# Attention in whole row groups instead of halves, in an encoder layer on one Trainium2 core

## The chip, the core and the metric

The kernel runs on one core of a Trainium2 chip. The core has a matrix engine (TensorE, PE in the profile; its weight loads are PEld), a vector engine (VectorE, DVE), a scalar engine (ScalarE, ACT), GpSimd (POOL) and a queue that issues DMA transfers (SyncE, SP). TensorE writes its results into PSUM, which has eight banks; VectorE and ScalarE read them from there, GpSimd works on SBUF. Each engine runs its own instructions in the order in which they were written, and waits at semaphores for the others. The metric is the device time of one execution in microseconds (us), the median of several runs.

## What is computed

One layer: RMS normalisation, a projection to queries, keys, values and a gate, neighbourhood attention on a grid of 32 rows by 64 columns, a SiLU gate, an output projection, the residual and a last normalisation. D_MODEL is 1024, SEQ 2048, with 16 heads of 64.

```python
h = rmsnorm(x, g)
q, k, v, gate = jnp.split(h @ w_in, 4, axis=-1)
# for each row r of the grid and each block of 16 columns: 8 rows x 32 columns of keys
s = jnp.einsum('bnqhd,bknjhd->bhnqkj', qr, kr) * scale
s = jnp.where(col_valid, s + bias, NEG_INF)
p = jax.nn.softmax(s, axis=-1)
o = jnp.einsum('bhnqkj,bknjhd->bnqhd', p, vr)
x = x + (o * jax.nn.silu(gate)) @ w_out
return rmsnorm(x, norm_f)
```

## The kernel before

**Stages.** The first half of the span is dense matrix products: values, and most of the projections in a seven-product scheme (`stage_one`, `stage_two`). Then comes attention, with the remaining dense matmuls fed in between its steps: first those of the projections (`projections`, lines 368 to 372, tiles `pp`), then those of the output projection (`outputs`, lines 1259 to 1263, tiles `po`). What is left of the output projection runs alone at the end. Dense products are made of three matmuls each, with operands split into a high and a low part.

**Attention's units.** Two heads are a pair p, eight pairs in all. The grid's rows are cut into four row groups T of eight rows; each sees the key rows `KEY_ROWS[T]`: 11, 15, 15 and 12 rows. The order is all pairs with T = 0, then for each pair T = 1 and T = 2, then all pairs with T = 3: 32 steps (p, T), called cycles below. Columns are cut into four groups C of 16 queries' columns with 24 or 40 key columns, the outer ones 24. A *half* is two column groups (0 and 1, or 2 and 3), so there are 64 halves, numbered i; N is 64.

**Steps of a half.** `scores(i)` makes 12 matmuls: two column groups, two heads, three products. Each head of a column group has a bank `s`. VectorE adds the table `EM` (bias and mask) and finds the largest value (line 1004, the masked sum), and ScalarE takes exponentials and their sums (line 1007). `normalise(i)` takes reciprocals on VectorE (line 1013) and scales on GpSimd (line 1015). `turns(i)` transposes the probabilities in 22 transposes of 64 x 64 results (line 1034) into two banks `ph` for each column group; ScalarE and VectorE copy these to SBUF tiles `pta` (lines 1037, 1038). `values(i)` makes 14 products, which the trace shows as 28 records (line 1052), into one bank `o` for each cycle. Behind a cycle's last half VectorE multiplies by the gate (line 1068) and the result is stored.

**The order around it.** The order is written out by hand. Step i of the loop at the end issues loads (`begin`), feeds dense matmuls in portions (`feed`, with `amount[i]` as the number of matmuls), and then one run without dense matmuls in it: `turns(i - 2)`, `scores(i)`, `values(i - 2)`, with `normalise(i - 1)` ahead of them. Later work (evacuations, stores, loads) stands in a list with a due time, counted in dense matmuls, and is issued when `due` passes it. A bank is handed out again when its readers are done, so a matmul that starts a new bank can wait for the copy of an older one.

**Tables.** `bias` (line 964) makes six tables `EM` for a pair on GpSimd, from two tiles `E` of bias rows (`load_e`, pool `ep`) and the mask. For T = 0 they change in each cycle, for T = 1 and 2 in every second one; for T = 3 they are loaded ready-made (`load_last`).

Of the kernel before, what the change touches and what calls it, by code (L numbers as in the profile page):

```python
# [69 lines left out]
def build(ctx, tc, x, xr, xt, wg, rpb, last, w_out, n0, nf, masks, out):  # L70
# [19 lines left out]
    qp = pool("qp", 4)  # L90
# [12 lines left out]
    pa = pool("pa", 2)  # L103
    mp = pool("mp", 6)
    ep = pool("ep", 4)
# [441 lines left out]

    X2 = {}
# [4 lines left out]
    def stage_one():  # L553
        us = [("k", j) for j in range(4)] + [(k, j) for j in range(4) for k in "qg"]
        X1 = {f: [(xs([128, 512], F32R, "h"), xs([128, 512], F32R, "l")) for _ in range(4)]
              for f in ("B12", "B11", "B21", "B22")}
        spot = mkp([128, 3, 512], F32, "spot")
        land = {f: [p([128, n], F32, "land")[:, :512] for _ in range(4)]
                for f, p, n in (("x12", kp, 960), ("x22", qp, 512), ("x11", vh, 512))}
        land["x21"] = [spot[:, k] for k in range(3)] + [lp([128, 512], F32, "land")]  # L560
        slots = [(mp, 512)] * 6 + [(ep, 512)] * 2 + [(sp, 512)] * 2 + [(pa, 768)] * 2 + [(vh, 512)] * 4
        slots += [(qp, 512)] * 4 + [(kp, 960)] * 4
# [4 lines left out]
        def split(f, t, k, scale=None):  # L567
            if f == "T1":
                X1.setdefault(f, []).append((xs([128, 512], F32R, "h"), xs([128, 512], F32R, "l")))
            elif f[0] == "T":  # L570
                X1.setdefault(f, []).append(tuple(p([128, n], F32R, "t")[:, :512] for p, n in (slots.pop(0), slots.pop(0))))
            split_to(*X1[f][k], t, scale and gain(scale, k))
# [191 lines left out]
    def stage_two():  # L764
        x12, x11, x21 = L2["x12"], L2["x11"], L2["x21"]
        x22 = [qp([128, 512], F32, "land") for _ in range(4)]
        for k in range(4):
            load_x(2, "x22", k, x22[k])
        slots = {"T2": [(mp, 512)] * 4 + [(kp, 960)] * 4,
                 "T3": [(sp, 512)] * 2 + [(pa, 768)] * 2 + [(qp, 512)] * 3 + [(lp, 512)],  # L770
                 "T4": [(vh, 512)] * 4 + [(mp, 512)] * 2 + [(ep, 512)] * 2}
# [65 lines left out]
        def form(f, x, *ks):  # L837
            def g():
                for k in ks:
                    h, l = (p([128, n], F32R, "t")[:, :512] for p, n in slots[f][2 * k:2 * k + 2])  # L840
# [126 lines left out]
    def load_last(p):  # L967
        if p % 2:
            ts = [mp([128, 512], F32, "em") for _ in range(6)]
        else:  # L970
            m = mkp([128, 3, 512], F32, "em")
            ts = [ep([128, 512], F32, "em") for _ in range(4)] + [m[:, 0], m[:, 1]]
# [11 lines left out]
    def scores(i):  # L984
# [14 lines left out]
        for C, pst in got:  # L999
            n = (r1 - r0) * width(C)  # L1000
            ST[i, C] = st = tiny.tile([128, 6], F32, name="st")
            X[i, C] = [xp([128, 512], F32, f"x{s}")[:, :n] for s in range(2)]
            for s in range(2):
                nc.vector.tensor_tensor_reduce(X[i, C][s], pst[s], EM[p, ROW_TYPE[T], COL_TYPE[C], s], -1.0, 1e38,  # L1004
                                               OP.add, OP.min, st[:, s:s + 1])
            for s in range(2):
                nc.scalar.activation(X[i, C][s], X[i, C][s], AF.Exp, bias=st[:, s:s + 1], scale=-1.0,  # L1007
                                     accum_out=st[:, 2 + s:3 + s])

    def normalise(i):  # L1010
        for C in pairs[i][2]:
            st = ST.pop((i, C))
            nc.vector.reciprocal(st[:, 4:6], st[:, 2:4])  # L1013
# [267 lines left out]
    first = 8  # L1281
# [141 lines left out]
```

## Time and profile before

| | |
|---|---|
| median of 3 runs | 1081.04 us (1079.96 to 1081.69) |
| the profiled execution | 1081.33 us, of which the span of its instructions is 1079.5 us |
| granted TensorE clock of that execution | 0.998 |
| dense stages, 0 to 535 us | TensorE busy 532.67 us |
| T = 0, 535 to 642 us | TensorE busy 105.83 us, GpSimd 64.36 us |
| T = 1 and 2, 642 to 870 us | TensorE busy 228.00 us, VectorE 159.78 us, ScalarE 147.44 us, GpSimd 114.88 us |
| T = 3, 870 to 1022 us | TensorE busy 151.69 us, VectorE 100.65 us |
| rest, 1022 to 1079.5 us | TensorE busy 49.80 us |

The span is divided by stages here, from a view that gives each engine's busy time in a stretch. Matmuls are pipelined and their ends are modelled: a record of a 512-column matmul is 0.39 us long while the next one starts 0.23 us after it, so start times say more than lengths. In a timeline several like records that follow each other are one row, with the start of the first and the end of the last.

### The profile page before, as it was taken

The page shows a single profiled execution, that of the slowest core. Times are in us where ns is not written, and L with a number is a line of the kernel's source. Part 1 is how long each engine was busy: PE and PEld are TensorE (multiplying, and loading weights), DVE is VectorE, ACT ScalarE, POOL GpSimd, SP SyncE. Part 2 cuts the span into 40 slices and gives each one's busy share as a digit, 9 for nine tenths or more (in the row PEclk, how much of TensorE's full clock was granted, in tenths as well). Part 3 has the DMA queues.
Part 4 walks back from the last instruction along what each step waited for, and adds up shares of the span by engine and source line. Part 5 has one row for each costly group of instructions (what it writes and reads, how often), then busy time and mean ns, then how long its engine had stood idle before and what let it go on. Part 6 is the DMA issues. An engine that isn't in the chain of part 4 may idle for free.

```text
span 1079.5 us, 21403 instructions
## 1 busy us (share of the span) xinstructions
PE 1068.0 (99%) x7621; PEld 872.9 (81%) x7621; DVE 721.4 (67%) x1695; ACT 520.1 (48%) x1245; POOL 278.4 (26%) x393
## 2 busy tenths in 40 slices
PE   9999999999999999999999999999999999999997
PEld 6888888887888888888878888888888888888885
DVE  5376888768897635566665667656777777676554
ACT  7545344333334334332366656665677655555321
POOL 0000222312321000000166665455445522222100
PEclk9999999999999999999999999999999999999999
DMA  8633555344545333424888777886888798876442
GB/s 304 223 98 101 191 203 183 126 133 138 175 132 150 109 88 102 162 96 143 275 254 274 216 241 232 256 253 193 259 291 261 211 284 276 257 240 203 133 147 78
DMA packets 129042, 207.59 MB, mean 192 GB/s; under 512 B 11752, under 2 KB 55272, under 8 KB 128936
## 3 DMA queue, kind: packets, MB, share of 16 engines
q1 hardware_dynamic: 128792, 205.97, 61.4%
q8 instruction: 60, 0.98, 0.4%
q14 instruction: 46, 0.38, 0.1%
q10 hardware_dynamic: 144, 0.26, 0.1%
HBM read 147.47 MB, written 58.72 MB: 191 GB/s over the span
## 4 chain that ended last, share of the span: by engine, by line
PE 95%; DVE 3%; ACT 1%; issue 1%; POOL 0%; DVEq 0%; POOLq 0%; ACTq 0%
PE pp L424 29%; PE pv L545 16%; PE o L1052 8%; PE s L997 8%; PE po L1263 6%; PE po L1259 6%; PE po L1261 5%; PE ph L1034 4%; PE pp L372 4%; PE pp L368 4%; PE pp L370 4%; DVE f L407 1%; PE zp L1278 1%; ACT x L1007 0%; DVE raw L413 0%
## 5 line engine op out<-in xcount | busy, mean ns | idle before, releaser
L1015 POOL TENSOR_SCALAR x<-x,st 128x360 f32<-128x360 f32 (+5 forms) x256 | 142.3, 575 | 270.2 <-DVE st L1013 225.0
L424 PE MATMUL pp<-h,f 128*128 128x512 f32 x576 | 186.3, 389 | 0.0
L1007 ACT ACTIVATE x<-x,st 128x360 f32<-128x360 f32 (+5 forms) x256 | 151.8, 594 | 50.3 <-DVE st L1004 50.1
L424 PE MATMUL pp<-t,f 128*128 128x512 f32 x648 | 156.0, 389 | 0.3 <-DVE u L437 0.2
L424 PEld LDWEIGHTS pp<-t,f 128*128 128x128 f32 x648 | 121.5, 188 | 26.3 <-DVE u L437 1.2
L444 POOL TENSOR_TENSOR tmp<-tmp,rb 128x512 f32<-128x512 f32 x36 | 58.5, 1626 | 271.8 <-DVE tmp L442 223.6
L1004 DVE CUSTOM_DVE_ANT_0 x<-s,em 128x360 f32<-128x360 f32 (+5 forms) x256 | 124.0, 540 | 3.9 <-PE s L997 2.6
L964 POOL TENSOR_TENSOR em<-e,mk 128x264 f32<-128x264 f32 (+3 forms) x94 | 77.1, 853 | 191.6 <-DVE u L437 189.8
L424 PEld LDWEIGHTS pp<-h,f 128*128 128x128 f32 x576 | 108.1, 188 | 22.3
L424 PE MATMUL pp<-l,f 128*128 128x512 f32 x288 | 112.0, 389 | 0.0
L1038 DVE COPY pta<-ph 120x384 f32<-120x384 f32 (+5 forms) x128 | 63.2, 517 | 66.6 <-PE ph L1034 66.2
L1037 ACT ACTIVATE pta<-ph 120x384 f32<-120x384 f32 (+5 forms) x128 | 52.1, 459 | 102.4 <-PE ph L1034 102.4
L1263 PE MATMUL po<-wol,gh 128*128 128x512 f32 x252 | 100.1, 397 | 0.0
L1259 PE MATMUL po<-woh,gh 128*128 128x512 f32 x252 | 99.4, 394 | 0.0
L1261 PE MATMUL po<-woh,gl 128*128 128x512 f32 x252 | 98.8, 392 | 0.0
L1052 PEld LDWEIGHTS o<-pta,vt 120*64 120x64 f32 (+2 forms) x1792 | 83.5, 137 | 18.5 <-issue 13.9
L1052 PE MATMUL o<-pta,vt 120*64 120x128 f32 (+5 forms) x1792 | 92.3, 254 | 0.3 <-ACT pta L1037 0.3
L545 PE MATMUL pv<-wh,h 128*128 128x512 f32 x256 | 88.2, 390 | 0.0
L545 PE MATMUL pv<-wh,l 128*128 128x512 f32 x256 | 87.9, 389 | 0.0
L545 PE MATMUL pv<-wl,h 128*128 128x512 f32 x256 | 87.9, 389 | 0.0
L997 PE MATMUL s<-kt,qh 64*128 64x480 f32 (+5 forms) x512 | 85.9, 377 | 1.2 <-DVE st L1004 1.0
L407 DVE TENSOR_TENSOR f<-raw,f 128x512 fp32r<-128x512 f32 x90 | 69.7, 775 | 22.4 <-ACT f L406 22.4
(147 smaller groups left out, 1874.4 us busy)
## 6 DMA issues: line engine op xcount, KB each, us to landing
raw<-in_wg_dram SPq DMA_DIRECT2D x126, 256.0 KB, 4.6
row<-in_xr_dram SPq DMA_DIRECT2D x32, 256.0 KB, 4.8
vd<-v SPq DMA_DIRECT2D x32, 256.0 KB, 2.9
k_hi<-hi SPq DMA_DIRECT2D x32, 256.0 KB, 3.0
k_lo<-lo SPq DMA_DIRECT2D x32, 256.0 KB, 3.1
sgd<-sg SPq DMA_DIRECT2D x32, 256.0 KB, 2.8
qr<-qd SPq DMA_DIRECT2D x32, 256.0 KB, 5.9
sgt<-sgd SPq DMA_DIRECT2D x32, 256.0 KB, 7.0
```

The costliest lines, as they stand in the source:

```text
L407: nc.vector.tensor_tensor(t[:, 1], src, t[:, 0].bitcast(F32), OP.subtract)
L424: nc.tensor.matmul(B[n, P], t[:, int(m == 2), c], x[k][int(m == 1)], start=P in (1, 6, 5) and k == 0 and m == 0, stop=k == 3 and m == 2, s ...
L545: nc.tensor.matmul(ps[t], a[:, o], b, start=k == 0 and m == 0, stop=k == NK - 1 and m == 2)
L964: (nc.gpsimd if attending[0] or not s else nc.vector).tensor_tensor(sh(t), E[p, s][:, u0 + 4:u1 + 4, v0 + 8:v1 + 8].rearrange("p u (s v) - ...
L997: nc.tensor.matmul(pst[s], qq[a, qs], kk[a, :r1 - r0, c0:c1].rearrange("p r (s c) -> p s r c", c=8), start=(m == 0), stop=(m == 2))
L1004: nc.vector.tensor_tensor_reduce(X[i, C][s], pst[s], EM[p, ROW_TYPE[T], COL_TYPE[C], s], -1.0, 1e38, OP.add, OP.min, st[:, s:s + 1])
L1007: nc.scalar.activation(X[i, C][s], X[i, C][s], AF.Exp, bias=st[:, s:s + 1], scale=-1.0, accum_out=st[:, 2 + s:3 + s])
L1015: nc.gpsimd.tensor_scalar(X[i, C][s], X[i, C][s], st[:, 4 + s:5 + s], 0.5, op0=OP.mult, op1=OP.mult)
L1052: nc.tensor.matmul(o[s * 64:s * 64 + 64, C * 128 + q0:C * 128 + q0 + nq], vt[:k, strip, s * 64:s * 64 + 64], t[:k, at:at + nq], start=firs ...
L1259: nc.tensor.matmul(p, gh, woh[q, j], start=(i == 0), stop=False)
L1261: nc.tensor.matmul(p, gl, woh[q, j], start=False, stop=False)
L1263: nc.tensor.matmul(p, gh, wol[q, j], start=False, stop=(i == NK - 1))
```

## The change

`turns`, `scores` and `values` of a whole cycle now stand in one run, and the loop goes over cycles m instead of halves i. Its run is: the transposes of both halves of cycle m - 1 (44), the scores of both halves of cycle m (24 matmuls), the values of both halves of cycle m - 1. The portion of dense matmuls between two runs is 28 for the first 25 steps and some 53 for the others, in place of 14 and 23 between two halves.

- The turned probabilities of a cycle lie in one tile `pta` of 3072 columns (`pt`, one buffer, in place of `pa` with two of 768). They come out of six banks: for each half two of 512 columns, one for each 64 queries, and two of 384 that both halves share. Each bank is copied whole, three by ScalarE and three by VectorE, so 96 copies by each in place of 128.
- `normalise` of a cycle's first half stands within `scores` of its second, between the masked sums of its two column groups; `normalise` of the second half stands 45% into the next portion of dense matmuls. Each takes one reciprocal for four sums in place of two.
- The table sums on GpSimd (`tables`) stand behind that normalising, 65% into the portion, in place of at its start. The pool of bias rows has two buffers in place of four, and the rows for the next tables are asked for behind the values of a run.
- Loads of keys, queries, values and gates have other places in the portion. `qp` has two buffers in place of four, and the first two stages use other tiles as landing places and operands (`xp`, the sixths of `pt`, `qp`).
- `run_roots` runs in each cycle.

```diff
     raw = pool("raw", 6)
     kp = pool("kp", 4)
-    qp = pool("qp", 4)
+    qp = pool("qp", 2)
     vp = pool("vp", 2)
     vhalf = []
...
     sp = pool("sp", 2)
     xp = pool("xp", 8)
     mkp = pool("mkp", 1)
-    pa = pool("pa", 2)
+    pt = pool("pt", 1)
     mp = pool("mp", 6)
-    ep = pool("ep", 4)
+    ep = pool("ep", 2)
+
+    def sixths():
+        t = pt([128, 3072], F32R, "sixths")
+        return [t[:, i * 512:i * 512 + 512] for i in range(6)]
+
...
               for f in ("B12", "B11", "B21", "B22")}
         spot = mkp([128, 3, 512], F32, "spot")
         land = {f: [p([128, n], F32, "land")[:, :512] for _ in range(4)]
-                for f, p, n in (("x12", kp, 960), ("x22", qp, 512), ("x11", vh, 512))}
+                for f, p, n in (("x12", kp, 960), ("x22", xp, 512), ("x11", vh, 512))}
+        sixth = sixths()
         land["x21"] = [spot[:, k] for k in range(3)] + [lp([128, 512], F32, "land")]
-        slots = [(mp, 512)] * 6 + [(ep, 512)] * 2 + [(sp, 512)] * 2 + [(pa, 768)] * 2 + [(vh, 512)] * 4
-        slots += [(qp, 512)] * 4 + [(kp, 960)] * 4
+        slots = [(mp, 512)] * 6 + [(qp, 512)] * 2 + [(sp, 512)] * 2 + sixth[:2] + [(vh, 512)] * 4
+        slots += sixth[2:] + [(kp, 960)] * 4
 
...
-    def scores(i):
+    def scores(i, between=None):
         p, T, cs = pairs[i]
         kh, kl = KT[p, T]
         qh, ql = QT[p, T]
@@ -996,72 +1007,109 @@
                     a = slice(s * 64, s * 64 + 64)
                     nc.tensor.matmul(pst[s], qq[a, qs], kk[a, :r1 - r0, c0:c1].rearrange("p r (s c) -> p s r c", c=8), start=(m == 0), stop=(m == 2))
             got.append((C, pst))
-        for C, pst in got:
+        ST[i] = st = tiny.tile([128, 12], F32, name="st")
+        for j, (C, pst) in enumerate(got):
             n = (r1 - r0) * width(C)
-            ST[i, C] = st = tiny.tile([128, 6], F32, name="st")
             X[i, C] = [xp([128, 512], F32, f"x{s}")[:, :n] for s in range(2)]
             for s in range(2):
+                o = 2 * j + s
                 nc.vector.tensor_tensor_reduce(X[i, C][s], pst[s], EM[p, ROW_TYPE[T], COL_TYPE[C], s], -1.0, 1e38,
-                                               OP.add, OP.min, st[:, s:s + 1])
+                                               OP.add, OP.min, st[:, o:o + 1])
+            if between and j == 0:
+                between()
             for s in range(2):
-                nc.scalar.activation(X[i, C][s], X[i, C][s], AF.Exp, bias=st[:, s:s + 1], scale=-1.0,
-                                     accum_out=st[:, 2 + s:3 + s])
+                o = 2 * j + s
+                nc.scalar.activation(X[i, C][s], X[i, C][s], AF.Exp, bias=st[:, o:o + 1], scale=-1.0,
+                                     accum_out=st[:, 4 + o:5 + o])
 
     def normalise(i):
-        for C in pairs[i][2]:
-            st = ST.pop((i, C))
-            nc.vector.reciprocal(st[:, 4:6], st[:, 2:4])
+        st = ST.pop(i)
+        nc.vector.reciprocal(st[:, 8:12], st[:, 4:8])
+        for j, C in enumerate(pairs[i][2]):
             for s in range(2):
-                nc.gpsimd.tensor_scalar(X[i, C][s], X[i, C][s], st[:, 4 + s:5 + s], 0.5, op0=OP.mult, op1=OP.mult)
+                o = 8 + 2 * j + s
+                nc.gpsimd.tensor_scalar(X[i, C][s], X[i, C][s], st[:, o:o + 1], 0.5, op0=OP.mult, op1=OP.mult)
 
     def split(C):
         return [b for b in strips(C) if b[3] == 128], [b for b in strips(C) if b[3] == 64]
 
-    def turns(i):
-        p, T, cs = pairs[i]
-        k = 8 * (KEY_ROWS[T][1] - KEY_ROWS[T][0])
-        for C in cs:
+
+
+    def places(m):
+        p, T = order[m]
+        put, at = {}, [1024, 1024]
+        for C in range(4):
             full, part = split(C)
-            halves_ = [full + [b for b in part if b[2] == 64 * h] for h in range(2)]
-            t = PT[i, C] = pa([128, 768], F32, "pta")
-            slots = t.rearrange("p (n h q) -> p h n q", h=2, q=64)
-            ph = [bank(384, f"ph{h}") for h in range(2)]
-            for j in range(3):
+            for b, blk in enumerate(full):
                 for s in range(2):
                     for h in range(2):
-                        if j < len(halves_[h]):
-                            o, at, q = j * 128 + s * 64, halves_[h][j][1] * k, slice(64 * h, 64 * h + 64)
-                            nc.tensor.transpose(ph[h][:k, o:o + 64], X[i, C][s][q, at:at + k], ident[q, q])
+                        put[C, blk[0], s, h] = C * 256 + b * 128 + s * 64
+            for blk in part:
+                for s in range(2):
+                    h = blk[2] // 64
+                    put[C, blk[0], s, h] = at[h]
+                    at[h] += 64
+        return put
+
+    def turns(m):
+        p, T = order[m]
+        k = 8 * (KEY_ROWS[T][1] - KEY_ROWS[T][0])
+        put = places(m)
+        PT[m] = t = pt([128, 3072], F32, "pta").rearrange("p (h c) -> p h c", h=2)
+        banks_ = {}
+
+        def copy(b):
+            w = (512, 512, 384)[b]
             for h in range(2):
-                n = len(halves_[h])
-                put = (lambda o, i_: nc.scalar.activation(o, i_, AF.Copy)) if h else nc.vector.tensor_copy
-                put(slots[:k, h, :2 * n], ph[h][:k, :128 * n].rearrange("p (n q) -> p n q", q=64))
+                (nc.vector.tensor_copy if h else lambda o, i_: nc.scalar.activation(o, i_, AF.Copy))(
+                    t[:k, h, b * 512:b * 512 + w], banks_[b, h][:k, :w])
+
+        for b in range(2):
+            for h in range(2):
+                banks_[b, h] = bank(512, f"ph{h}")
+            if b == 0:
+                banks_[2, 0], banks_[2, 1] = bank(384, "ph0"), bank(384, "ph1")
+            lists = [[], []]
+            for C in (2 * b, 2 * b + 1):
+                full, part = split(C)
+                for blks in (full, part):
+                    for blk in blks:
+                        for s in range(2):
+                            for h in range(2):
+                                if (C, blk[0], s, h) in put:
+                                    lists[h].append((put[C, blk[0], s, h], C, s, blk[1] * k))
+            for h in range(2):
+                lists[h].sort()
+            for n in range(max(len(l) for l in lists)):
+                for h in range(2):
+                    if n < len(lists[h]):
+                        o, C, s, at = lists[h][n]
+                        q = slice(64 * h, 64 * h + 64)
+                        nc.tensor.transpose(banks_[o // 512, h][:k, o % 512:o % 512 + 64], X[2 * m + b, C][s][q, at:at + k], ident[q, q])
+                if n == 7:
+                    copy(b)
+        copy(2)
 
     def values(i):
         p, T, cs = pairs[i]
         k = 8 * (KEY_ROWS[T][1] - KEY_ROWS[T][0])
+        put = places(i // 2)
         if cs[0] == 0:
             O[p, T] = bank(512, "o")
         o = O[p, T]
         vt = VT[p, T]
+        t = PT[i // 2]
         for C in cs:
             X.pop((i, C))
-
-        def product(C, s, blk, t, at, first, last):
-            strip, _, q0, nq = blk
-            nc.tensor.matmul(o[s * 64:s * 64 + 64, C * 128 + q0:C * 128 + q0 + nq],
-                             vt[:k, strip, s * 64:s * 64 + 64], t[:k, at:at + nq],
-                             start=first, stop=last, skip_group_check=True)
-
-        for C in cs:
             full, part = split(C)
-            for b, blk in enumerate(full):
+            for b, (strip, _, q0, nq) in enumerate(full + part):
                 for s in range(2):
-                    product(C, s, blk, PT[i, C], b * 256 + s * 128, b == 0, False)
-            for h, blk in enumerate(part):
-                for s in range(2):
-                    product(C, s, blk, PT[i, C], 512 + s * 128 + blk[2], False, h == len(part) - 1)
-            del PT[i, C]
+                    h = slice(q0 // 64, (q0 + nq) // 64)
+                    at = put[C, strip, s, h.start]
+                    to = o[s * 64:s * 64 + 64, C * 128 + q0:C * 128 + q0 + nq]
+                    nc.tensor.matmul(to.rearrange("d (h q) -> d h q", q=64) if nq > 64 else to,
+                                     vt[:k, strip, s * 64:s * 64 + 64], t[:k, h, at:at + 64] if nq > 64 else t[:k, h.start, at:at + 64],
+                                     start=b == 0, stop=b == len(full + part) - 1, skip_group_check=True)
...
-    early = 96 * (12 - len(units_two)) + 192
-    first = 8
-    kept = 60
-    amount = [(early - kept - 3 * first) / 48] * 48 + [(384 + kept - 30) / 18] * 18
-    calm_debt = amount[0] / 2
-    for i in range(3):
-        amount[i] += first
+    cycles = len(order)
+    dense, end_of_it = 28.0, 24
+    amount = [dense] * 25
+    first = 16
+    amount[0] -= first / 2
+    amount[1] += first
+    calm_debt = dense / 4
+    amount += [(96 * (12 - len(units_two)) + 546 - sum(amount) - first - end_of_it) / (cycles - 25)] * (cycles - 25) + [end_of_it]
     fill = projections()
     outs = outputs()
...
-    def begin(i):
+    def next_sums(m):
+        return next((n for n in range(m + 1, cycles) if order[n][1] < 2), None)
+
+    def begin(m):
         all_loads()
-        m = i // 2
         quiet[0] = True
-        if i % 2 == 0 and i < N:
-            p, T = order[m]
-            load_v(p, T)
-            ty = ROW_TYPE[T]
+        if m >= 1:
+            later_loads([lambda: load_sg(*order[m - 1])], 1, 0)
+        if m < cycles:
+            later_loads([lambda: load_v(*order[m])], 4, 0)
+        if m + 1 < cycles:
+            nx = order[m + 1]
+            if nx[1] == 3:
+                later_loads(load_last(nx[0]), 12, 1.5)
+            later_loads(load_k(*nx), 14 if nx[1] < 3 else 22, 5)
+        if m == 0:
+            bias(0, 0, 2)
+            later_loads(load_e(order[1][0]), 5, 3)
+
+    def middle(m):
+        if 1 <= m < cycles:
+            split_q(*order[m])
+        if m + 1 < cycles:
+            later_loads([load_q(*order[m + 1])], 1, 0)
+
+    def tables(m):
+        p, T = order[m]
+        ty = ROW_TYPE[T]
+        if (p, ty, 0, 0) not in EM:
             for cty in range(3):
-                if (p, ty, cty, 0) not in EM:
-                    bias(p, ty, cty)
-                    quiet[0] = i == 0
-            if m + 1 < len(order):
-                nx = order[m + 1]
-                kh, kl = load_k(*nx)
-                if nx[1] == 3:
-                    later_loads(load_last(nx[0]), 1, 1.5)
-                elif nx[0] != p:
-                    later_loads(load_e(nx[0]), 5, 3)
-                later_loads([kh, kl], 9, 4)
-        if i % 2 == 0 and 2 <= i <= N:
-            p, T = order[m - 1]
-            later_loads([lambda: load_sg(p, T)], 15, 0)
-
-    def middle(i):
-        m = i // 2
-        if i % 2 and m + 1 < len(order):
-            split_q(*order[m + 1])
-        if i == 0 or i % 2 and m + 2 < len(order):
-            later_loads([load_q(*order[m + (2 if i else 1)])], 1, 0)
+                bias(p, ty, cty)
+            quiet[0] = False
 
     stage_one()
     stage_two()
     attending[0] = True
-    for i in range(N + 2):
-        a = amount[i]
-        begin(i)
-        feed(a * 0.25)
-        if quiet[0]:
-            run_roots()
+    for m in range(cycles + 1):
+        a = amount[m]
+        begin(m)
+        feed(a * 0.15)
+        run_roots()
+        feed(a * 0.15)
+        middle(m)
+        feed(a * 0.15)
+        if m:
+            normalise(2 * m - 1)
         feed(a * 0.2)
-        middle(i)
-        feed(a * 0.55, 8)
-        if 0 < i <= N:
-            normalise(i - 1)
-        if i > 1:
-            turns(i - 2)
-        if i == N + 1:
+        if m < cycles:
+            tables(m)
+        feed(a * 0.35, 8)
+        if m:
+            turns(m - 1)
+        if m == cycles:
             all_loads()
             feed(6)
-        if i < N:
-            scores(i)
-        if i > 1:
-            values(i - 2)
+        else:
+            scores(2 * m)
+            if m == 0:
+                feed(first, 8)
+            scores(2 * m + 1, lambda: normalise(2 * m))
+        if m:
+            values(2 * m - 2)
+            values(2 * m - 1)
+        n = next_sums(m)
+        if 0 < m and n and order[m][1] < 2:
+            for f in load_e(order[n][0]):
+                f()
```

18 lines of the change are left out of this document (11 added, 7 removed).

## The prediction

> **What bounds the kernel now.** I read the page's busy times first, then its clock row and its chain of waits.
>
> ```profile
> span 1079.5 us, 21403 instructions
> PE 1068.0 (99%) x7621; PEld 872.9 (81%) x7621; DVE 721.4 (67%) x1695; ACT 520.1 (48%) x1245; POOL 278.4 (26%) x393
> PEclk9999999999999999999999999999999999999999
> PE 95%; DVE 3%; ACT 1%; issue 1%; POOL 0%; DVEq 0%; POOLq 0%; ACTq 0%
> ```
>
> TensorE is busy throughout, at full clock, and is 95% of the chain that ended last. So the time is the length of TensorE's own stream. The change neither adds nor removes a matmul, so its worth lies in how that stream is cut up. I therefore read the timeline of TensorE around one attention run of the middle stage (T = 1, 2); columns are start, length, engine, line, tiles, count.
>
> ```profile
> 747.64 0.39 PE L370 MATMUL pp<-l,w 128*128 128x512 f32 x1
> 747.87 0.39 PE L372 MATMUL pp<-h,w 128*128 128x512 f32 x1
> 748.19 0.80 PE L1034 MATMUL ph<-ident,x 64*120 64x64 f32 x20
> 748.91 0.74 PE L997 MATMUL s<-kt,qh 64*128 64x480 f32 x3
> 750.00 0.45 PE L997 MATMUL s<-kt,ql 64*128 64x360 f32 x2
> 750.38 1.44 PE L1052 MATMUL o<-pta,vt 120*64 120x128 f32 x28
> 751.43 0.39 PE L1052 MATMUL o<-pta,vt 120*64 120x128 f32 x5
> 751.75 0.50 PE L368 MATMUL pp<-h,w 128*128 128x512 f32 x1
> 752.09 0.40 PE L370 MATMUL pp<-l,w 128*128 128x512 f32 x1
> L1052 PE MATMUL o<-pta,vt 120*64 120x64 f32 x384 | 21.9, 221 | 0.0
> ```
>
> Dense matmuls follow each other every 0.23. The run takes 752.09 - 747.87 - 2 x 0.23 = 3.76 us beyond the dense stream. No engine wait stands in these rows, yet there are seams:
> - Entering: a dense matmul would have started at 748.10; the first transpose starts at 748.19: 0.09.
> - Leaving: the last five records of the values start at 751.43 and end at 751.82. A last one of 0.22 starts at 751.60, some 0.04 after the one before it. The first dense matmul starts 0.15 after it, and the second one 0.34 later instead of 0.23: 0.11 + 0.11 = 0.22.
> - Scores to values: the second score starts at 748.91 and the eleventh at 750.00, so 0.121 each; eleven would end at 750.24, and the values start 0.14 after that. The neighbouring run has the narrow column group first:
>
> ```profile
> 741.93 0.60 PE L997 MATMUL s<-kt,qh 64*128 64x360 f32 x3
> 742.91 0.56 PE L997 MATMUL s<-kt,ql 64*128 64x480 f32 x2
> 743.40 1.44 PE L1052 MATMUL o<-pta,vt 120*64 120x128 f32 x28
> ```
>
> There it is 0.109 each, and 743.40 - 741.93 - 11 x 0.109 = 0.27. A mean step overstates the seam where the wide group is last and understates it where it is first; their mean, 0.20, is what I use. From transposes to scores I see no seam.
>
> **The change, part by part.** *One run for two halves.* Before, 62 runs hold transposes, scores and values; in the changed program's order 31 runs hold 44, 24 and 28 products (56 records) with the same matmuls around them, and the dense total is the same. Each of the 31 saves one set of seams. Middle stage: 0.09 + 0.20 + 0.22 = 0.51. The first and last stage, one run each:
>
> ```profile
> 616.66 0.50 PE L997 MATMUL s<-kt,qh 64*128 64x264 f32 x3
> 617.40 0.42 PE L997 MATMUL s<-kt,ql 64*128 64x352 f32 x2
> 617.76 1.44 PE L1052 MATMUL o<-pta,vt 88*64 88x128 f32 x28
> 897.66 0.63 PE L997 MATMUL s<-kt,qh 64*128 64x384 f32 x3
> 898.55 0.39 PE L997 MATMUL s<-kt,ql 64*128 64x288 f32 x2
> 898.88 1.44 PE L1052 MATMUL o<-pta,vt 96*64 96x128 f32 x28
> ```
>
> T = 0, narrow first: 0.082 each, seam 0.20, less the 0.07 that the middle stage shows for this order: 0.13, in all 0.44. T = 3, wide first: 0.099 each, seam 0.13, plus 0.07: 0.20, in all 0.51. The first step among the transposes may be longer than the others too, by 0 to 0.05. I take 0.55, 0.47 and 0.54. With 16, 7 and 8 runs of scores: 8.8 + 3.3 + 4.3 = 16.4 us. Bounds: with the scores' seam at its smaller reading of 0.13 and no more, 13.5; with 0.27 and the long first step, 20. The last transposes and values, merged too, give 0.5.
>
> *Six banks and three wide copies on each engine, new waits.* All eight banks come around within a run: six turned banks, eight of scores and one of values, beside the dense one under way. In the new order each bank of scores after the first waits for a copy out of a turned bank, in turn ScalarE and VectorE. The last waits for the first masked sum on VectorE, and the values wait for the second. The copies of before:
>
> ```profile
> L1037 ACT ACTIVATE pta<-ph x128: 370/487/497, 549.5 to 1019.8; 120x384 f32<-120x384 f32 x48, 88x384 f32<-88x384 f32 x24, 96x384 f32<-96x384 f32 x24, 120x256 f32<-120x256 f32 x16
> L1038 DVE COPY pta<-ph x128: 400/547/558, 550.4 to 1019.9; 120x384 f32<-120x384 f32 x48, 88x384 f32<-88x384 f32 x24, 96x384 f32<-96x384 f32 x24, 120x256 f32<-120x256 f32 x16
> 748.79 1.02 DVE L1038 COPY pta<-ph 120x384 f32<-120x384 f32 x2 [1.47 <-PE ph L1034]
> 748.88 0.77 ACT L1037 ACTIVATE pta<-ph 120x384 f32<-120x384 f32 x2 [2.42 <-PE ph L1034]
> 750.04 0.66 DVE L1004 CUSTOM_DVE_ANT_0 x<-s,em 128x480 f32<-128x480 f32 x1 [0.23 <-PE s L997]
> 751.20 0.53 DVE L1004 CUSTOM_DVE_ANT_0 x<-s,em 128x360 f32<-128x360 f32 x1
> 751.65 0.53 DVE L1004 CUSTOM_DVE_ANT_0 x<-s,em 128x360 f32<-128x360 f32 x1
> ```
>
> 256 to 384 columns costs 0.117 on ScalarE and 0.147 on VectorE; a 512-wide copy is then 0.60 and 0.69 (estimates), each next one starting 0.08 earlier. 22 transposes take 748.91 - 748.19 = 0.72, a pair about 0.06. Before, twelve transposes are issued within 0.33 of the first, and copies start 0.27 (VectorE) and 0.36 (ScalarE) behind that. Now sixteen take 0.45. Times from the first transpose, T = 1, 2: ScalarE copies 0.81-1.41, 1.50-2.10, 2.02-2.50; VectorE 0.72-1.41, 1.41-2.10, 2.02-2.57; masked sums from 2.5 every 0.45 or 0.58. Transposes end at 1.43. First scores (360) 1.43-2.0: their second head needs 1.41, no wait. Second group needs ScalarE's second copy at 2.10, plus hand-over: wait 0.1. Third needs 2.50, has time until 2.75. Fourth, at 3.4, needs the first masked sum at 3.1. Values, at 4.0, need 3.5. So 0.1 per run. With T = 0 and 3 the first scores end 0.1 to 0.15 sooner against the same copies: 0.25. New waits: 16 x 0.1 + 15 x 0.25 = 5.4 us. Bounds: none, and 0.5 in each run, 15.5.
>
> [...]
>
> *Normalising and table sums moved.* The second half of a cycle is now normalised 12.6 dense matmuls (2.9 us) behind the run, and the table sums stand on GpSimd's queue behind it.
>
> ```profile
> 750.74 0.69 ACT L1007 ACTIVATE x<-x,st 128x480 f32<-128x480 f32 x1 [1.09 <-DVE st L1004]
> 752.11 0.58 ACT L1007 ACTIVATE x<-x,st 128x360 f32<-128x360 f32 x1
> 752.69 0.58 ACT L1007 ACTIVATE x<-x,st 128x360 f32<-128x360 f32 x1
> 747.45 2.39 POOL L1015 TENSOR_SCALAR x<-x,st 128x360 f32<-128x360 f32 x4 [4.20 <-DVE st L1013]
> 749.80 5.50 POOL L964 TENSOR_TENSOR em<-e,mk 128x360 f32<-128x360 f32 x6
> e<-in_rpb_dram SPq DMA_DIRECT2D x18, 240.0 KB, 5.0
> ```
>
> Exponentials are 0.69 and 0.58 apart: from 3.2, eight end at 8.3. The run ends at 2 x 3.76 - 0.55 + 0.1 = 7.1, normalising starts at 10.0 and ends at 12.4. The next run's transposes start at 7.1 + 28 x 0.23 = 13.5, and those of the second half at 14.2: 1.8 spare. The table sums end at 17.9, 0.92 apart, the first at 13.3; the masked sums use them from 16.0 to 20: 2 spare. Cost nothing; without that cover each microsecond late is one on TensorE, in 31 runs for normalising and 15 for tables. The reciprocal between masked sums waits for ScalarE's fourth exponential, and holds up two masked sums on VectorE; their banks are needed only by dense groups and later transposes, microseconds on. Loads of keys, queries, values and gates keep their count, stand in another order on SyncE's queue, and are asked for about a cycle ahead; one that waits there holds up only others for the next cycle. The bias rows have two buffers instead of four, so their load waits for the table sums of the cycle before, about 3 us into its run; 5.0 us later they are there, some 2 us before GpSimd turns to them. Landing buffers of the first two stages change place, with no dense matmul's operand waiting for another engine than before: nothing.
>
> Sum: 1081.3 (the profiled execution: span 1079.5 and 1.8 around it; 0.3 above the median shown) - 16.4 - 0.5 + 5.4 = 1069.8, and 1069.5 beside the median.
>
> **The rivals.** *A, evacuation eats most of it.* VectorE has three copies (1.9) and eight masked sums (4.1) in a run, and if the copies start late, behind leftovers of the dense stage, every bank of scores is late. The rows' idle times of 1.47 and 2.42 before the copies speak against it, the eight-bank round for it. At the bound of 0.5 per run: 1081.3 - 16.9 + 15.5 = 1080; at half of the excess 1075. [...]
> *B, slower: bias rows or table sums late.* Place: the first masked sum of the 15 cycles that change tables. It decides once the rows land over 4 us later than planned (2 spare before GpSimd, 2 behind it). A stall of 0.8 x 15 = 12 us takes the gain away; at 2 us each: 1069.5 + 30 = 1099; at 1.2, 1087. Against it: the median of 5.0.
> *C, the change does not do what it says:* the seams are tied to the work, say because the second half's scores and values drain as before. Then only entering and leaving are saved, 31 x 0.31 = 9.6, against 5.4 of waits: 1077.
>
> **How the numbers follow.** Forecast 0.60, with its own range 1061 (20.5 saved, no waits) to 1073 (16.9 saved, 9 of waits); 13.5 saved with 11 of waits would be 1079, which I count under A. A 0.16, C 0.06, B 0.18. A measurement of this kernel can tell some 0.2% (2.2 us) from no change: the upper third of A falls within that. So faster 0.60 + 0.06 + 0.10 = 0.76, same 0.06, slower 0.18. The range 1061 to 1082 takes in A and C, and leaves out most of B.
>
> **What would show it.** Right: 31 runs, of about 7.1 us in the middle stage, with score rows starting right behind the transposes and one gap before the values; dense steps still 0.23. Wrong: waits of scores on copies above 0.3 per run (A), idle TensorE at the transposes on GpSimd, or masked sums waiting for table sums (B); a run of twice 3.5 with no wait listed (C).

## The result and the profile after

| | before | after |
|---|---|---|
| time, median (range), us | 1081.2 (1080.0 to 1081.7) | 1067.3 (1066.6 to 1067.7) |
| ratio of after to before, 95% interval | | 0.9872 (0.9855 to 0.9889) |
| span of the profiled execution, us | 1079.5 | 1065.1 |
| attention runs with transposes, scores and values | 62 | 31 |

The change saves 14.0 us. The forecast was 1069.5. From the page of after, the rows that answer to those of before (span; busy times; TensorE's granted clock; chain of waits by engine):

```profile
span 1065.1 us, 21027 instructions
PE 1052.9 (99%) x7621; PEld 879.5 (83%) x7621; DVE 715.3 (67%) x1599; ACT 516.5 (48%) x1213; POOL 288.1 (27%) x393
PEclk9999999999999999999999999999999999999998
PE 91%; DVE 4%; ACT 1%; POOL 1%; issue 1%; DMA 1%; POOLq 0%; DVEq 0%; ACTq 0%
```

TensorE still sets the end, with as many matmuls (7621) at the same granted clock (0.997, for 0.998 before). But its share of the chain fell from 95% to 91%, and GpSimd stands there with 1% where it had 0%: a wait has come in. First one undisturbed run, from TensorE's timeline (start, length, engine, line, tiles, count):

```profile
776.27 0.39 PE L375 MATMUL pp<-l,w 128*128 128x512 f32 x1
776.59 1.50 PE L1088 MATMUL ph<-ident,x 64*120 64x64 f32 x44
777.91 0.73 PE L1008 MATMUL s<-kt,qh 64*128 64x360 f32 x4
778.33 0.49 PE L1008 MATMUL s<-kt,ql 64*128 64x360 f32 x2
...
780.58 0.34 PE L1008 MATMUL s<-kt,ql 64*128 64x360 f32 x1
780.86 2.67 PE L1110 MATMUL o<-pta,vt 120*64 120x128 f32 x56
783.45 0.50 PE L377 MATMUL pp<-h,w 128*128 128x512 f32 x1
783.79 0.40 PE L373 MATMUL pp<-h,w 128*128 128x512 f32 x1
```

44 transposes, 24 scores and 56 records of values stand in one run. Beyond the dense stream it takes 783.79 - 776.27 - 2 x 0.227 = 7.07 (planned 7.1), where two runs of before took 2 x 3.77 = 7.54. The entering seam is still 0.09 (776.27 + 0.23 to 776.59), the last score to the values 0.28, but each occurs once. The same reading for all stages, with typical runs of each, in us:

| stage (runs) | two runs before | one after | saved |
|---|---|---|---|
| T = 0 (7) | 6.72 | 6.40 | 0.32 |
| T = 1, 2 (16) | 7.54 | 7.06 | 0.48 |
| T = 3 (8) | 6.92 to 7.02 | 6.55 | 0.42 |

That is 2.2 + 7.7 + 3.4 = 13.3 us. Some runs are longer than these. Over all attention runs of the two traces the sum goes from 235.3 to 222.9: 12.4 saved.

One cause of the longer runs shows among the waits of TensorE's weight loads (waiting line, releaser: us in total, times, longest):

```profile
PEld ph L1088 <- POOL x L1031: 7.5, 21, 0.5
PEld o L1110 <- DVE st L1016: 5.1, 21, 0.3
PEld s L1008 <- ACT pta L1064: 1.0, 5, 0.3
```

Transposes wait for GpSimd's normalising, which the prediction had done 1.8 us early. The third row is the scores' wait for copies, where only the last part of it is listed. The second row is no wait that costs: it names the last to release the values, in the seam before them, and with dense matmuls put into that place (below) it grows to 7.8 while the values start 0.09 behind these. The worst run, from the timelines of VectorE and of all engines around its start:

```profile
812.99 1.29 DVE L1175 TENSOR_TENSOR gl<-ograw,gh 128x512 fp32r<-128x512 f32 x2 [1.17 <-ACT gh L1174]
814.20 0.68 DVE L190 TENSOR_TENSOR wol<-raw,woh 128x512 fp32r<-128x512 f32 x1
814.80 0.68 DVE L515 SCALAR_TENSOR_TENSOR ql<-qr,qh 128x512 fp32r<-128x512 f32 x1
815.40 0.68 DVE L1206 TENSOR_TENSOR y<-po,xr 128x512 f32<-128x512 f32 x1
816.00 0.68 DVE L190 TENSOR_TENSOR wol<-raw,woh 128x512 fp32r<-128x512 f32 x1
...
816.60 0.17 DVE L1027 RECIPROCAL st<-st 128x4 f32<-128x4 f32 x1
816.96 2.82 POOL L1031 TENSOR_SCALAR x<-x,st 128x480 f32<-128x480 f32 x4 [4.07 <-ACT xr L1209]
...
817.40 0.97 PE L1088 MATMUL ph<-ident,x 64*120 64x64 f32 x24
...
818.75 0.81 PE L1088 MATMUL ph<-ident,x 64*120 64x64 f32 x8 [0.38 <-POOL x L1031]
...
819.83 0.51 PE L1088 MATMUL ph<-ident,x 64*120 64x64 f32 x10 [0.27 <-POOL x L1031]
```

GpSimd has been idle for 4.07 us, and the second half's exponentials were done long before; this is the last of them on ScalarE's timeline:

```profile
812.25 0.19 ACT L1022 ACTIVATION_READ_ACCUMULATOR x<-x,st 128x1 f32 x1
```

So from 812.4 to 816.6 the normalising waits for nothing but its reciprocal's turn on VectorE. That stands behind six operations: two splits of gated rows, two of output weights, one of queries and an evacuation, most of which the output projection brings into the same portion of the cycle. GpSimd starts 0.4 before the run's first transpose, where the prediction had it done 1.8 before those of the second half; the transposes take 2.84 from first to last start instead of 1.29. Six runs are longer in their transposes, by 3.6 us in sum. As whole runs these six are 3.2 longer than in the version below that normalises at once.

### The profile page after: what moved, and what is told of

Read it like the earlier page. It is cut to its first block, busy times and chain, and to the rows that moved or that the text cites. A ratio compares the mean times of both kernels' runs of the same rounds, so it can differ in the third digit from the quotient of the medians.

```text
span 1065.1 us, 21027 instructions
## 1 busy us (share of the span) xinstructions
PE 1052.9 (99%) x7621; PEld 879.5 (83%) x7621; DVE 715.3 (67%) x1599; ACT 516.5 (48%) x1213; POOL 288.1 (27%) x393
## 4 chain that ended last, share of the span: by engine, by line
PE 91%; DVE 4%; ACT 1%; POOL 1%; issue 1%; DMA 1%; POOLq 0%; DVEq 0%; ACTq 0%
PE pp L429 29%; PE pv L550 16%; PE o L1110 7%; PE s L1008 7%; PE po L1309 5%; PE po L1311 5%; PE po L1307 5%; PE ph L1088 4%; PE pp L377 4%; PE pp L373 3%; PE pp L375 3%; DVE f L412 1%; POOL x L1031 1%; ACT x L1022 1%; PE zp L1326 1%
## 5 line engine op out<-in xcount | busy, mean ns | idle before, releaser
L1031 POOL TENSOR_SCALAR x<-x,st 128x360 f32<-128x360 f32 (+5 forms) x256 | 151.4, 610 | 250.3 <-DVE st L1027 218.6
L429 PE MATMUL pp<-t,f 128*128 128x512 f32 x480 | 121.8, 390 | 0.3 <-DVE u L442 0.2
L429 PEld LDWEIGHTS pp<-t,f 128*128 128x128 f32 x480 | 90.0, 188 | 19.8 <-DVE u L442 1.2
L1064 DVE COPY pta<-ph 120x512 f32<-120x512 f32 (+5 forms) x96 | 58.0, 641 | 71.3 <-PE ph L1088 71.2
L1064 ACT ACTIVATE pta<-ph 120x512 f32<-120x512 f32 (+5 forms) x96 | 49.7, 558 | 80.1 <-PE ph L1088 80.1
L1110 PEld LDWEIGHTS o<-pta,vt 120*64 120x64 f32 (+2 forms) x1792 | 80.9, 137 | 7.5 <-DVE st L1016 5.1
L1110 PE MATMUL o<-pta,vt 120*64 120x128 f32 (+5 forms) x1792 | 85.3, 253 | 0.0
```

The lines of the kernel that those rows point to most:

```text
L429: nc.tensor.matmul(B[n, P], t[:, int(m == 2), c], x[k][int(m == 1)], start=P in (1, 6, 5) and k == 0 and m == 0, stop=k == 3 and m == 2, s ...
L1031: nc.gpsimd.tensor_scalar(X[i, C][s], X[i, C][s], st[:, o:o + 1], 0.5, op0=OP.mult, op1=OP.mult)
L1064: (nc.vector.tensor_copy if h else lambda o, i_: nc.scalar.activation(o, i_, AF.Copy))(t[:k, h, b * 512:b * 512 + w], banks_[b, h][:k, :w])
L1110: nc.tensor.matmul(to.rearrange("d (h q) -> d h q", q=64) if nq > 64 else to, vt[:k, strip, s * 64:s * 64 + 64], t[:k, h, at:at + 64] if n ...
```

## The experiments

Theory: the gain is one set of seams per cycle less the scores' waits for copies, and some 3 us are given back because the second half's reciprocal stands too late on VectorE's queue. Rivals: the seams are a wait in disguise; the copies have slack; the loss sits elsewhere. The edits of the first four are made to the changed kernel.

**Normalising earlier.**

```diff
         feed(a * 0.15)
+        if m:
+            normalise(2 * m - 1)
         run_roots()
...
-        feed(a * 0.15)
-        if m:
-            normalise(2 * m - 1)
-        feed(a * 0.2)
+        feed(a * 0.35)
```

> The second half of a cycle is normalised after 15% of the dense portion instead of 45%, ahead of the splitting of queries and of the rows' roots; nothing else changes. Theory (the transposes of the second half wait for GpSimd in some six cycles, because VectorE's reciprocal stands behind the dense work's own operations): the runs of 7.25 to 8.5 us go back to about 7.05, and the time falls from 1067.3 by 2.5 to 4 us, to 1063.5 to 1065. Rival (the cost sits elsewhere, and a reciprocal that is asked for earlier waits for the exponentials and holds up evacuations of dense banks behind it on VectorE): 1067 to 1071, with waits of dense matmuls on VectorE.

Measured 1064.6 (1063.9 to 1065.4), 2.7 below the changed kernel. Waits of the weight loads:

```profile
PEld ph L1088 <- POOL x L1031: 2.5, 7, 0.4
```

The 7.5 has become 2.5; transposes of one run are still late (0.5 us), where six were. There is no new wait of dense matmuls for VectorE (those of the tiles `pp` are 1.1 us, for 1.2). As the theory said.

**Table sums ahead of normalising.**

```diff
+        if m < cycles:
+            tables(m)
         if m:
             normalise(2 * m - 1)
         feed(a * 0.2)
-        if m < cycles:
-            tables(m)
```

> On GpSimd the table sums are issued just ahead of normalising the second half instead of behind it; nothing else changes. Theory (normalising has about 1.8 us to spare before the transposes want it): in the 15 cycles that change tables it comes 4.3 to 5.5 us later, the transposes of the second half wait 2 to 4 us each, and the time rises by 30 to 50 us, to 1097 to 1117. Rival (the spare is larger than worked out, or the masked sums set the place of both): within 3 us of 1067.3, and then the order of the two on GpSimd's queue was worth nothing.

Measured 1107.4 (1106.4 to 1108.7): 40 us above the changed kernel, and above the kernel before. One of the runs, on TensorE's timeline:

```profile
771.77 0.91 PE L1088 MATMUL ph<-ident,x 64*120 64x64 f32 x22
774.33 0.27 PE L1088 MATMUL ph<-ident,x 64*120 64x64 f32 x2 [1.65 <-POOL x L1031]
774.98 0.39 PE L1088 MATMUL ph<-ident,x 64*120 64x64 f32 x6 [0.37 <-POOL x L1031]
```

The first half's transposes go through, the second half's wait; transposes take up to 5.6 us in a run. From first transpose to first score the runs are 31.5 us longer in sum than in the changed kernel. Another 7.9 lies behind that, in the scores, and almost all of it in the seven runs whose transposes wait longest (2.4 us or more). In or right behind these waits the granted clock falls to 0.50 for 3.4 us, once for 6.8 (807.4 to 814.2 us), and the scores of these runs take 0.8 to 1.7 longer; no other run of this trace shows it. The whole execution's clock is 0.986, for 0.997 in the changed kernel. So about a fifth of the 40 us goes with a slower TensorE behind the wait, and is not the wait itself. That part of the change, the order on GpSimd, is needed by the rest of it: there is no room for the table sums ahead of the normalising.

**Dense matmuls between scores and values**, and **between the two halves' scores.**

```diff
-        feed(a * 0.35, 8)
+        feed(a * 0.15, 8)
...
         if m:
+            feed(a * 0.2)
             values(2 * m - 2)
```

> 20% of each cycle's dense portion (5 to 6 matmuls in most cycles) is put between the scores and the values; the dense total is the same. Theory (each switch between dense and tiled matmuls on TensorE costs 0.09 going in and 0.2 to 0.25 coming out, and the waits on copies are small): 31 more switches cost 31 x 0.3 = 9 us less the 0.22 to 0.28 of the gap between scores and values where it goes away, so 1069 to 1077. Rival (the gap before the values and the scores' bank waits are a wait on VectorE's masked sums and copies, not a switch): the dense matmuls cover it, 1060 to 1066.

```diff
-        feed(a * 0.35, 8)
+        feed(a * 0.15, 8)
...
-            feed(6)
+            feed(6 + a * 0.2)
         else:
             scores(2 * m)
...
+            feed(a * 0.2)
             scores(2 * m + 1, lambda: normalise(2 * m))
```

> 20% of each cycle's dense portion (5 to 6 matmuls in most cycles) is put between the scores of the first and of the second half; the transposes, the values and the dense total stay. Theory (seams, not evacuation, are what one run saves): one more leaving and entering per cycle, 31 x 0.3 to 0.5 = 9 to 15 us, so 1076 to 1082, about all of what the change won. Rival (scores wait for copies of turned banks and for masked sums, and the dense matmuls would cover that): 1064 to 1069.

Measured 1082.4 and 1090.5: both more than the theory allowed, by 5.4 and 8.5 us. The runs show two costs. For T = 1, 2 their parts are longer by 0.21 to 0.24 (scores and values apart) and by 0.40 to 0.42 (scores apart) than one whole run: 30 cycles with the insertion x 0.23 = 6.9, and 30 x 0.41 = 12.3. And the transposes take 9.2 and 10.7 us longer in sum than in the changed kernel, from first to last start; the likely reason is that the portion that was moved is the one behind normalising. The waits of the weight loads, scores and values apart:

```profile
PEld ph L1088 <- POOL x L1031: 12.6, 35, 0.7
```

Together 16.1 and 23.0, against 15.2 and 23.3 between the medians. To part the two costs, the split of the scores was made again on top of the early normalising. The edits that follow are made to that version (1064.6).

> The early normalising (15% of the portion) with 20% of each cycle's dense portion between the scores of the two halves, so that what follows the seam has GpSimd's work done in time. Theory (the 23 us that splitting cost before were 12.5 of seams, 31 x 0.41 by the runs' lengths in that trace, and 10 of transposes waiting for a normalising that the split had pushed nearer to them): with the waits gone it costs the seams alone, 1064.6 + 12.5 = 1077, between 1075 and 1079. Rival (the split itself makes the scores wait, whatever GpSimd does): 1083 to 1088.

Measured 1079.0 (1078.5 to 1080.2): at the theory's upper end, below the rival. One cycle on TensorE's timeline:

```profile
782.94 0.39 PE L375 MATMUL pp<-l,w 128*128 128x512 f32 x1
783.25 1.50 PE L1088 MATMUL ph<-ident,x 64*120 64x64 f32 x44
784.57 0.74 PE L1008 MATMUL s<-kt,qh 64*128 64x360 f32 x4
...
785.68 0.60 PE L1008 MATMUL s<-kt,ql 64*128 64x480 f32 x2
786.22 0.49 PE L377 MATMUL pp<-h,w 128*128 128x512 f32 x1
786.55 0.39 PE L373 MATMUL pp<-h,w 128*128 128x512 f32 x1
...
787.25 0.39 PE L373 MATMUL pp<-h,w 128*128 128x512 f32 x1
787.56 0.76 PE L1008 MATMUL s<-kt,qh 64*128 64x480 f32 x4
...
789.07 2.67 PE L1110 MATMUL o<-pta,vt 120*64 120x128 f32 x56
...
792.00 0.39 PE L377 MATMUL pp<-h,w 128*128 128x512 f32 x1
```

From 782.94 to 792.00 there are 9.06; seven dense steps of 0.227 in it (five between the halves, two behind) leave 7.47, against 7.07 for a whole run: 0.40 for one more leaving and entering, with no wait listed. In this kernel the dense matmuls came between the halves in 28 cycles: 28 x 0.41 = 11.5 of the 14.5; late transposes in three runs make another 2.1, and one wait of scores near 754 us 0.8. So the seam is TensorE's own price, not a wait that dense work would cover.

**One more copy on ScalarE.**

```diff
             w = (512, 512, 384)[b]
+            if b == 0:
+                nc.scalar.activation(t[:k, 0, 0:512], banks_[0, 0][:k, :512], AF.Copy)
```

> The early normalising, with ScalarE copying the first turned bank twice: one more copy of 512 columns, about 0.5 us after the first, ahead of its second and third. Theory (the scores' second group and those after it wait for these copies as they come, with 0.1 to 0.25 of wait per run now): each run waits 0.4 to 0.5 more, 31 runs give 12 to 16, so 1077 to 1081. Rival (the copies have slack, and the runs of scores are simply as long as their matmuls): at most 3 us, 1064 to 1068.

Measured 1079.1 (1077.8 to 1079.4). The weight loads of scores in this kernel, from the groups by line:

```profile
L1008 PEld LDWEIGHTS s<-kt,qh 64*128 64x128 f32 x512 | 66.1, 187 | 17.8 <-ACT pta L1066 9.4 <-DVE st L1016 1.3 <-issue 0.7
```

The copies' share of their idle time went from 1.1 to 9.4 us, which is again only the last part of each wait, and a run of T = 1, 2 is 0.5 longer (7.57 for 7.06). The copies have no slack here: of an added one of 0.59 us, 0.47 per run go into the time.

**Reciprocal and normalising of the first half behind all masked sums.**

```diff
-            if between and j == 0:
-                between()
...
+        if between:
+            between()
```

> The early normalising, with the first half's reciprocal and normalising behind all four masked sums of the second half, not between them. Theory (the two masked sums that VectorE holds up behind the reciprocal free banks that nothing wants for some microseconds, and GpSimd has the time): within 1 us of 1064.6. Rival 1 (that stop of VectorE costs TensorE something): 1060 to 1063. Rival 2 (GpSimd's chain of normalising and table sums has no slack, and starting 1 us later moves all of it): 1068 to 1090, with transposes or masked sums waiting for GpSimd.

Measured 1066.6 (1065.8 to 1066.6): 2.0 more, between the theory and its second rival. Transposes are late in four runs instead of one (1.9 us for 0.5 in sum); the attention runs of the trace are 0.8 longer in all, so 1.2 of the 2.0 isn't accounted for. Those four runs show that GpSimd's series has no whole microsecond to give there; that VectorE's stop at the reciprocal costs TensorE something is not borne out.

**Normalising at once, the changed kernel again, and one table sum on VectorE.** The first puts normalising ahead of the whole portion:

```diff
+        if m:
+            normalise(2 * m - 1)
         feed(a * 0.15)
-        if m:
-            normalise(2 * m - 1)
```

> The second half's normalising right behind the run, at 0% of the dense portion instead of 15%. Theory (at 15% nearly all of the transposes' waits are gone, and what is left, 0.2 to 0.5 us in five runs, comes from masked sums waiting for table sums): VectorE now stands up to 1.3 us at the reciprocal until the exponentials are done, and nothing on TensorE wants it then: 1063.5 to 1065.5. Rival (operands of dense matmuls or evacuations queued behind the reciprocal are late): 1066 to 1075, with dense matmuls waiting for VectorE.

> The changed kernel as it is, beside the next one on the same chip. Theory (its time was 1067.3 and the early normalising's gain is no matter of the chip it ran on): 1066.5 to 1068, some 3 us above the version that normalises at once. Rival: under 1065.5, and then that gain was a difference between chips or runs.

The last is made to the version that normalises at once:

```diff
-            (nc.gpsimd if attending[0] or not s else nc.vector).tensor_tensor(
+            (nc.gpsimd if (attending[0] and (cty or not s)) or not s else nc.vector).tensor_tensor(
```

> Normalising at once (1064.1), with one of the six table sums of a cycle on VectorE instead of GpSimd. Theory (the runs that are still 0.25 to 0.4 too long, near 640, 790, 829 and 875 us, wait for masked sums that wait for GpSimd's table sums; GpSimd's series then ends 0.9 sooner): those go to the length of their neighbours, 1.0 to 1.3 us in all, 1062.8 to 1063.3. Rival (the sum on VectorE waits there for its bias rows or for GpSimd's buffer, and dense evacuations behind it are late): 1065 to 1080.

Normalising at once: 1064.1 (1063.9 to 1064.4), the changed kernel again 1067.2 (1066.6 to 1067.5), one sum on VectorE 1063.6 (1063.2 to 1064.8). The last two ran on one chip and are 3.6 apart, with both edits in the second, so a gain of some 3 us is no matter of the chip. For normalising at once, the chain of waits (page) and the transposes' weight loads (groups by line):

```profile
PE 95%; DVE 3%; issue 1%; DMA 1%; ACT 0%; POOL 0%; DVEq 0%; POOLq 0%; ACTq 0%
```

```profile
L1088 PEld LDWEIGHTS ph<-ident,x 64*120 64x120 f32 (+2 forms) x1408 | 42.4, 128 | 11.3 <-issue 8.5 <-POOL em L974 2.5 <-POOL x L1031 0.4
```

TensorE is back at 95% of the chain, no run's transposes are late, and the attention runs sum to 219.6: 3.3 less than in the changed kernel. The sum on VectorE takes 0.2 each out of the runs near 640 and 829, as expected, but not the 0.4 near 790 and only 0.1 of the 0.26 near 875, and one near 969 is 0.2 longer with it. Near 790, on the timeline of the version that normalises at once, VectorE's first copy starts 1.08 after the first transpose instead of 0.75, behind two weight splits (near 875 it is 1.19 instead of 0.72), which points to the copies and not to GpSimd:

```profile
789.89 1.28 DVE L190 TENSOR_TENSOR wol<-raw,woh 128x512 fp32r<-128x512 f32 x2
...
790.01 1.50 PE L1088 MATMUL ph<-ident,x 64*120 64x64 f32 x44
...
791.09 1.74 DVE L1064 COPY pta<-ph 120x512 f32<-120x512 f32 x3
```

At 1063.6 it misses the 1062.8 to 1063.3 of its theory, and its 0.5 in the median lies within the ranges of the two, so whether it gains is open. Normalising at once beats both kernels, at 0.984 of the time before (0.9822 to 0.9857).

## Why the prediction was right, step by step

- *TensorE's stream sets the end.* Right: the same 7621 matmuls at a clock of 0.997, for 0.998, and what was saved or lost shows as the length of runs.
- *Seams, 16.4 us.* Slightly too small. The runs' saving and the scores' waits (next point) give 0.58 for T = 0, 0.59 for T = 1, 2 and 0.63 for T = 3, so 4.1 + 9.4 + 5.0 = 18.5, for 0.47, 0.55 and 0.54. One thing that the sum lacked shows in the trace: the first step of the values is 0.16 where later ones of its width are 0.11, and it is now paid once. So 56 records take 2.44 from first to last start, no more than 2 x 1.22; that is 0.05 a run, some 1.5 in all. The transposes take 1.21 or 1.29 from first to last start where two halves took 2 x 0.66 or 2 x 0.70, 0.11 less per run. But in the kernel before, for T = 1, 2, the first score starts ahead of a half's last transposes, 0.61 after the first one, and 2 x 0.61 is less than the 1.32 of now; so how much of that 0.11 is a gain, beside the 0 to 0.05 that the sum held, stays open. I had planned 24 pair steps; 44 transposes of two heads go in 22, and 22 x 0.06 is the 1.32 from the first transpose to the first score. That the seams are a price of TensorE (against rival C) the splits show: 0.21 to 0.24 for one more leaving behind scores and entering to values, 0.40 to 0.42 between two halves of scores.
- *Waits of scores on copies, 5.4 us.* Right, as far as typical runs tell. In the split kernel the second half's scores have free banks: their 11 steps take 0.90, 1.22 and 0.98 (T = 0; 1, 2; 3). 23 such steps would be 1.88, 2.55 and 2.05; in whole runs they are 2.14, 2.66 and 2.26. So 0.26, 0.11 and 0.21 (forecast 0.25, 0.1, 0.25): 7 x 0.26 + 16 x 0.11 + 8 x 0.21 = 5.3. That the copies set this pace is what the extra copy shows. The widths were worked out well too; this is the view of one tile (min/median/max in ns):

```profile
L1064 ACT ACTIVATE pta<-ph x96: 474/594/603, 551.2 to 1004.5; 120x512 f32<-120x512 f32 x32, 88x512 f32<-88x512 f32 x16, 120x384 f32<-120x384 f32 x16, 96x512 f32<-96x512 f32 x16
L1064 DVE COPY pta<-ph x96: 541/686/692, 551.2 to 1004.7; 120x512 f32<-120x512 f32 x32, 88x512 f32<-88x512 f32 x16, 120x384 f32<-120x384 f32 x16, 96x512 f32<-96x512 f32 x16
```

  0.594 and 0.686, for 0.60 and 0.69.
- *Normalising costs nothing, 1.8 us spare.* This is the step that failed, in 6 of 31 runs. It held for the steady cycles, which show no wait, and counted the exponentials and GpSimd's own time, but not the queue of VectorE in front of the reciprocal, 4.2 us long at the worst place. It was mis-sized by 3.2 us, as the lengths of these six runs tell; the early normalising wins 2.7 of the time back and the normalising at once 3.1.
- *Table sums cost nothing, 2 us spare.* Nearly: 0.2 to 0.3 in two runs. The bias rows, rival B's point, were in time: GpSimd's sums wait 1.2 us for them in the whole trace. But behind rival B stood a real cliff: with the two series on GpSimd swapped it costs 40 us.
- *Rival A* (copies late behind leftovers of the dense stage) happens in one run, near 790, for 0.4.
- *The sum.* Regular runs save 13.3, the last transposes and values 1.0 (forecast 0.5: 5.33 in three runs becomes 4.36 in two). Longer runs cost some 1.7 more than the longer ones of before: 4.1 now, 3.2 of it the late normalising, for 2.3 then, which the prediction had not counted. That is 12.6, for the 12.4 read from the traces; the forecast had 11.5. Too small were the seams by 2.1 and the end by 0.5, and left out were 2.3 of gain and 4.1 of loss. That these nearly cancel is luck: the mechanism was right but for the normalising, and the closeness of the forecast does not show that its terms were.

The rest is 14.4 of span less 12.4. Of it 1.1 lies in the first matmuls of the program, which the change doesn't touch, and which is told below; how much of that is in the medians stays open. The other 1.0 lies in the dense steps between the runs. What these take beyond 0.227 each is 2.2 in sum before and 1.2 after, nearly all in the first ten steps behind a run (0.233 on average in the first three of them after the leaving seam), and the change halves the number of runs. So this, too, is a price of alternating, 0.03 a run, and the prediction had no term for it.

## What to carry over

Where TensorE alternates between full and narrow tiles at 99% busy, count its alternations: 0.4 to 0.6 us each here, paid on TensorE and not covered by other work, so the longer runs paid. How near the evacuating copies are to setting the pace here, the extra one shows: of its 0.59 us, 0.47 went into each run. When runs are merged, ask for each producer of the next run not only how long it takes but which queue its smallest instruction stands in: a reciprocal of 0.17 us behind six dense operations made transposes late by up to 1.5 us in a run. And place it right behind what it depends on, even if its engine then stands still for a while: with normalising at once VectorE stands 16.8 us in all at its 64 reciprocals, for 1.1 in the changed kernel, and the time is 3.1 less.

## What the hardware showed beside this

The program starts with 21 small matmuls that wait for one tile of zeros from GpSimd (1.90 us in both traces) and for nothing else. TensorE's timeline, before and after:

```profile
1.90 7.28 PE L1278 MATMUL zp<-z 128*128 128x512 bf16 x21 [1.90 <-POOL z L1275]
```

```profile
1.90 6.17 PE L1326 MATMUL zp<-z 128*128 128x512 bf16 x21 [1.90 <-POOL z L1323]
```

They start 0.43 apart and then change to 0.22: after 12 steps in the one execution, after 7 in the other, which is 1.1 us of the difference between the two spans. The trace's records of the granted clock begin at 7.1 and 4.9 us, just where the spacing changes. What the clock was before that is not shown, as there is no record of it. In the other profiles the change comes after 6 to 14 steps, in one of the changed kernel itself after 6. So spans of two profiled executions are compared here to some 1.5 us at best; the length of runs inside them is compared to hundredths.

The seam behind scores is larger than that behind values. In the split kernel, from the last start of scores to the second dense start there is 0.46 beyond a dense step (T = 1, 2), 0.12 of it the last score's own step; behind values it is 0.26, 0.04 of it the last record's.
